# One decoder layer on one core: head squares in four column strips, a priority on the turned keys, and a merge written into the tail of the last scan group

## The chip, the cores and the metric

The kernel runs on one core of a Trainium2 chip. The metric is the device time of one execution in microseconds (us); lower is better.

## The reference

One layer of a hybrid decoder is computed in float32 for a prompt of 512 tokens and for 8 samples of 8 tokens each (576 tokens together), with shared weights:

```python
h = x + 0.5 * swiglu(rmsnorm(x), ffn1)                  # 1024 -> 2816 -> 1024
z, xbc, dt, q, k, v, f, g_ssd, g_att = split(rmsnorm(h) @ w_in)
y_ssd = SSD(z, conv(xbc), dt)                           # 32 heads of 64, 4 groups, state 128
q = rmsnorm(q per head of 64);  k = rmsnorm(k per head of 64)   # 16 query heads, 4 key heads
y_att = attention(q, k_all, v_all, bias from cumsum(log_sigmoid(f)))   # samples: + 2048 cached rows
merged = sigmoid(g_ssd) * (y_ssd @ w_ssd_proj) + sigmoid(g_att) * (y_att @ w_attn_proj)
h = h + merged @ w_out
y = h + 0.5 * swiglu(rmsnorm(h), ffn2)
```

Besides `y`, the keys, values, log forgets and the states of the scan and the convolution are outputs.

## The kernel before

Activations lie turned: 128 features on the partitions, the 576 tokens along the free axis, and eight such tiles make the 1024 features. Each large product is taken in three terms by `mm3` (lines 204 to 210): weights and activations are split in a high part and a remainder of type float32r (`split` and `hilo`; the high part is copied on ScalarE, the remainder subtracted on VectorE, or for some weights on GpSimd), and three matmuls of 128x288 are issued for each 128 rows of the contraction. `acc()` gives such a product a PSUM bank: from two banks called `acc`, and where `wide` is set also from two called `pv`.

A scheduler sets the order on each engine: it simulates the written program and gives each engine one fixed list, in which a block under `soon()` has a higher priority. Within the attention loop the order on TensorE is that of the code (`manual_schedule`). Engines follow their lists strictly; a DMA issue that waits for a buffer holds up what stands behind it on its queue (ScalarE's and GpSimd's DMAs stand in the lists of those engines). Pools hand out tiles by tag; a tile of a tag with `bufs=n` waits until the n-th tile before it is no longer read, and a new pool's tile waits for the tiles whose memory it takes over.

The stages in order of time, with the lines that the change touches:

- FFN 1, until about 470 us.
- Keys, queries and values, 480 to 580 us. Each of ten tiles (2 of keys, 8 of queries; each holds two heads of 64 rows) goes through `squares` (651): ScalarE squares it into `sq`, and two matmuls with a 20-column selector `hE` add the two heads' sums to rows 2j and 2j+1 of `hp_` (512 prompt columns) and `hq_` (64 sample columns). When all ten are in, the 20 rows are turned, their inverse roots are taken on VectorE and turned back into `hr` (20 x 576).
- Heads are scaled by a matmul of `hr` with a selector `sel` that GpSimd copies out of the identity (`heads`, 662): lines 670 and 747 for the keys, 776 for the samples' part of the eight query tiles. These selectors take turns in four buffers.
- Attention, 620 to 900 us. The samples' cached keys `kk` are turned on TensorE (907) and copied to `kT` on ScalarE (908); the scores read them (917). Between these steps `fill()` puts slices of other projections.
- The convolution and four scan groups, 900 to 1390 us. `conv_tile` evicts a projection into `xr` (two buffers) and works on it. Of group g, `group_out` multiplies the scan's output by 512 rows of `w_ssd_proj`: for each of eight tiles j and two halves, twelve matmuls, then VectorE scales the result (`u`, line 1378) and adds it to `accs[j]` (1380).
- The merge, from 1392 us: for each j, two loads (`th` and `mt`, 1403 and 1405), VectorE's `th = (th + 1) * accs[j]` (1406), GpSimd's `th += mt` (1407; VectorE for j = 7), ScalarE's high part `mh` (217), VectorE's remainder `ml` (218). `th` and `mt` come from the pool `mg`, whose memory belongs to the scan's pools before. Then the product with `w_out` (eight tiles, each over all eight `mh` and `ml`) is added to the residual `hts`, which was loaded on ScalarE's queue (1410), and FFN 2 follows, until the end.

Of the kernel before, what the change touches and what calls it, by code (L numbers as in the profile page):

```python
# [48 lines left out]
for _n, _w in (("id", P), ("one", P), ("mT", P), ("smT", NS), ("sgn", 1),  # L49
               ("ev", 1), ("od", 1), ("kb", 4), ("hE", 38), ("scan", NT), ("sm", B * NS), ("rq", 4), ("page", P), ("cm", P)):  # L50
    COFF[_n] = (_o, _w)
    _o += _w
# [3 lines left out]
def constants():  # L56
# [17 lines left out]
    put("kb", ((i[:, None] % 32) // T == np.arange(4)[None]) * 1.0)  # L74
    put("hE", (np.arange(38)[None] == 18 + i[:, None] // 64) * 1.0)
    t = np.arange(NT)
# [17 lines left out]
def build(ctx, tc, A, O):  # L94
# [544 lines left out]
    with pool("att", side="right", reuse_waits="tile") as ap:  # L639
# [9 lines left out]
        nhead = [0]  # L649

        def squares(kf):
# [6 lines left out]
            mm(hp_[:20], lhsT=w, rhs=sq[:, :NP], start=j == 0, stop=j == 9)  # L658
            mm(hq_[:20, :NS], lhsT=w, rhs=sq[:, NP:], start=j == 0, stop=j == 9)

        def heads(j, tag="bias", bufs=4):

            sel = tl(ap, [20, 2, 64], tag=tag, bufs=bufs)
            G.tensor_copy(sel, ident[:20, 2 * j:2 * j + 2].unsqueeze(2).to_broadcast([20, 2, 64]))
            return sel.rearrange("k e m -> k (e m)")
# [56 lines left out]
        vtok = tokens(vf, O["v_p"], O["v_s"], "vt")  # L722
        hr = tl(ap, [20, NT], tag="hr")
        V.tensor_scalar(hr[:, :NP], hp_[:20], 1.0 / 64, EPS, ALU.mult, ALU.add)
        V.tensor_scalar(hr[:, NP:], hq_[:20, :NS], 1.0 / 64, EPS, ALU.mult, ALU.add)

        t = tr()
# [3 lines left out]
        xr_ = tl(ap, [P, 100], tag="pb", bufs=2)  # L731
        V.tensor_copy(xr_, t[:, :100])
        yr = rsqrt(xr_, 100, ap, (("L", 4), ("PT", 2), ("Ls", 7)))
        t = tr()
        for c in range(4):
            nc.tensor.transpose(t[:20, c * P:(c + 1) * P], yr[:, c * 20:(c + 1) * 20], ident)
        V.tensor_copy(hr[:, :NP], t[:20])
        t = tr()
        nc.tensor.transpose(t[:20, :P], yr[:, 80:100], ident)
        V.tensor_copy(hr[:, NP:], t[:20, P - NS:P])  # L740
        khat, khs, sels = kfs, [], []
# [30 lines left out]
        for j in range(8):  # L772
            sel = heads(2 + j)
            if j == 0:
                headnorm(qt[0], sel, 64)
            mm(t[:, j * NS:(j + 1) * NS], lhsT=sel, rhs=hr[:, NP:], start=True, stop=True)
# [10 lines left out]
        newb = tl(ap, [P, B, NS], tag="newb")  # L787
        cn = tl(ap, [P, NS], tag="cn")
        nc.scalar.dma_start(out=cn, in_=ap3(cumD, 32 * NT + NP, [(NT, 16), (0, T), (1, NS)]))
# [92 lines left out]
        class Sample:  # L882
# [17 lines left out]
            def turn_keys(self, jq):  # L900
                kk = self.kk.pop(jq)
                self.kT = []
                for p in range(2):
                    self.kT.append(tl(ap, [P, 512], tag="kT", bufs=2))
                    t = tr()
                    for i in range(4):
                        nc.tensor.transpose(t[:, i * P:(i + 1) * P], kk[:, i, p * P:(p + 1) * P], ident)  # L907
                    act(self.kT[p], t, AF.Copy)

# [187 lines left out]


    xzs = ExitStack()
    xz = xzs.enter_context(pool("xz", side="right", reuse_waits="tile"))  # L1100
# [90 lines left out]

    sa = mixes.enter_context(pool("ssdacc", reuse_waits="tile"))
    with xzs, pool("ssd", side="right", reuse_waits="tile") as wk:
        accs = [tl(sa, [P, NT], tag=f"accs{j}") for j in range(8)]
# [12 lines left out]
        def group_scan(g, bT, cT, xg):  # L1207
# [21 lines left out]
            def halves(half):  # L1229

                for i in range(4):
                    if half == 0:
                        yhl.append((tl(wk, [P, NT], F32R, tag="ygh", bufs=4), tl(wk, [P, NT], F32R, tag="ygl", bufs=4)))
# [130 lines left out]
        def group_out(g, ysq, ys_):  # L1364
# [3 lines left out]
            for j in range(8):  # L1368
                w = cw.get(j)
                for half in range(2):  # L1370
# [5 lines left out]
                    else:  # L1376
                        u = tl(wk, [P, HT], tag="u", bufs=2)
                        V.tensor_tensor(u, a, rg[:, hs(half)], ALU.mult)
                        E = V if g == 3 else G
                        E.tensor_tensor(accs[j][:, hs(half)], accs[j][:, hs(half)], u, ALU.add)  # L1380

        gs = Cols(win, CGS)
        late = iter(range(8))
        for g in range(4):
# [11 lines left out]
    hp2 = ctx.enter_context(pool("h2", side="right", reuse_waits="tile"))  # L1396
    hts = [tl(hp2, [P, NT], tag=f"h{k}") for k in range(8)]
    with mixes:
        with pool("mhl", bufs=8, side="right", reuse_waits="tile") as mp, pool("mg", side="right", reuse_waits="tile") as mg:
            mhl = []  # L1400
            for j in range(8):
                th = tl(mg, [P, NT], tag="th", bufs=3)
                nc.sync.dma_start(out=th, in_=thD[:, 8 + j, :])
                mt = tl(mg, [P, NT], tag="mt", bufs=3)
                nc.scalar.dma_start(out=mt, in_=mattD[:, j, :])
                V.scalar_tensor_tensor(th, th, 1.0, accs[j], ALU.add, ALU.mult)
                (G if j < 7 else V).tensor_tensor(th, th, mt, ALU.add)
                mhl.append(hilo(mp, th, "mh", "ml"))
            for j in range(8):
                nc.scalar.dma_start(out=hts[j], in_=hD[:, j, :])  # L1410
            wide[0] = True
            co = Cols(A["w_out"][0], 0)
            nrm3 = Norm(16, mg)
            for j in range(8):
                w = co.get(j)
                for half in range(2):
                    a = acc()
                    mm3(a, w, mhl, half)
                    hv = hts[j][:, hs(half)]
                    with soon():  # L1420
                        V.scalar_tensor_tensor(hv, a, 0.5, hv, ALU.mult, ALU.add)
                nrm3.add(hts[j])
            nrm3.finish()
            share[0] = 0

# [50 lines left out]
```

## Time and profile before

| | us |
|---|---|
| three runs | 1902.23, 1907.57 (median), 1909.16 |
| profiled execution | 1901.34, of which the span is 1899.5 |
| TensorE busy in the span | 1843.6 (97%) |
| VectorE, ScalarE, GpSimd busy | 1061.9, 745.5, 603.7 |
| mean clock that the throttle granted to TensorE | 0.987 |

PE is TensorE (PEld its weight loads), DVE VectorE, ACT ScalarE, POOL GpSimd, SP the engine that only issues DMAs; a "q" behind a name is an engine's queue. A busy PE is counted by its matmuls' durations, which overlap: neighbours among the 128x288 matmuls start 0.13 us apart and are listed with 0.29 us. "Granted clock" is the share of full speed that TensorE was allowed in a stretch.

### The profile page before, as it was taken

The page shows a single profiled execution, that of the slowest core. Times are in us where ns is not written, and L with a number is a line of the kernel's source. Part 1 is how long each engine was busy: PE and PEld are TensorE (multiplying, and loading weights), DVE is VectorE, ACT ScalarE, POOL GpSimd, SP SyncE. Part 2 cuts the span into 40 slices and gives each one's busy share as a digit, 9 for nine tenths or more (in the row PEclk, how much of TensorE's full clock was granted, in tenths as well). Part 3 has the DMA queues.
Part 4 walks back from the last instruction along what each step waited for, and adds up shares of the span by engine and source line. Part 5 has one row for each costly group of instructions (what it writes and reads, how often), then busy time and mean ns, then how long its engine had stood idle before and what let it go on. Part 6 is the DMA issues. An engine that isn't in the chain of part 4 may idle for free.

```text
span 1899.5 us, 38775 instructions
## 1 busy us (share of the span) xinstructions
PE 1843.6 (97%) x15335; PEld 1738.3 (92%) x15335; DVE 1061.9 (56%) x2308; ACT 745.5 (39%) x1545; POOL 603.7 (32%) x678
## 2 busy tenths in 40 slices
PE   7999999999999999999899999999979999999999
PEld 7999999999899888888898898888979999999998
DVE  5544234443425677776746968787665545445442
ACT  4233223333323555554425645555423333223322
POOL 0432002312312334433224644747434322102210
PEclk9999999999998999999999999999989999999999
DMA  5453443444625678785456445344543444444432
GB/s 153 111 142 123 134 128 118 122 140 140 158 80 147 187 225 244 213 227 155 115 134 190 148 126 144 104 133 123 165 144 109 132 128 139 132 139 123 121 116 69
DMA packets 298235, 269.71 MB, mean 142 GB/s; under 512 B 55068, under 2 KB 262092, under 8 KB 297900
## 3 DMA queue, kind: packets, MB, share of 16 engines
q1 hardware_dynamic: 230864, 186.52, 35.0%
q10 hardware_dynamic: 57828, 46.09, 7.9%
q0 software_dynamic: 9360, 34.61, 5.9%
q8 instruction: 121, 1.98, 0.4%
q14 instruction: 62, 0.51, 0.1%
HBM read 223.71 MB, written 38.73 MB: 138 GB/s over the span
## 4 chain that ended last, share of the span: by engine, by line
PE 85%; DVE 5%; DMA 4%; ACT 3%; issue 1%; POOL 1%; ACTq 1%; SPq 0%; POOLq 0%; DVEq 0%
PE acc L208 17%; PE acc L209 16%; PE acc L210 16%; PE pv L209 7%; PE pv L208 7%; PE pv L210 7%; PE tr L917 2%; PE tr L907 1%; PE mm L844 1%; DMA ab<-cumD 1%; PE pv L875 1%; PE mm L862 1%; PE pv L1299 1%; DVE kf L1140 1%; PE pv L955 1%
## 5 line engine op out<-in xcount | busy, mean ns | idle before, releaser
L173 ACT ACTIVATE whi<-stage 128x512 fp32r<-128x512 f32 (+2 forms) x474 | 294.8, 622 | 739.4 <-PE acc L209 650.5
L208 PE MATMUL acc<-xh,whi 128*128 128x288 f32 x1792 | 544.7, 304 | 9.0 <-ACT tt L1129 3.8
L209 PE MATMUL acc<-xl,whi 128*128 128x288 f32 x1792 | 535.8, 299 | 0.0
L210 PE MATMUL acc<-xh,wlo 128*128 128x288 f32 x1792 | 535.0, 299 | 0.0
L174 DVE TENSOR_TENSOR wlo<-stage,whi 128x512 fp32r<-128x512 f32 (+1 forms) x373 | 261.1, 700 | 263.3 <-ACT whi L173 249.4
L208 PEld LDWEIGHTS acc<-xh,whi 128*128 128x128 f32 x1792 | 341.1, 190 | 15.4 <-ACT tt L1129 6.7
L209 PEld LDWEIGHTS acc<-xl,whi 128*128 128x128 f32 x1792 | 341.3, 190 | 1.9 <-issue 1.4
L210 PEld LDWEIGHTS acc<-xh,wlo 128*128 128x128 f32 x1792 | 340.7, 190 | 1.8 <-issue 1.2
L174 POOL TENSOR_TENSOR wlo<-stage,whi 128x512 fp32r<-128x512 f32 (+1 forms) x101 | 138.2, 1368 | 315.8 <-ACT whi L173 300.4
L341 POOL TENSOR_TENSOR u<-u,s 128x288 f32<-128x288 f32 x88 | 81.3, 924 | 425.6 <-DVE u L340 379.9
L208 PE MATMUL pv<-xh,whi 128*128 128x288 f32 (+1 forms) x720 | 214.1, 298 | 1.0 <-ACT xh L220 0.9
L209 PE MATMUL pv<-xl,whi 128*128 128x288 f32 (+1 forms) x720 | 212.9, 296 | 0.0
L210 PE MATMUL pv<-xh,wlo 128*128 128x288 f32 (+1 forms) x720 | 212.4, 295 | 0.0
L208 PEld LDWEIGHTS pv<-xh,whi 128*128 128x128 f32 (+1 forms) x720 | 135.1, 188 | 1.7 <-ACT xh L220 1.1
L209 PEld LDWEIGHTS pv<-xl,whi 128*128 128x128 f32 (+1 forms) x720 | 135.1, 188 | 1.2
L210 PEld LDWEIGHTS pv<-xh,wlo 128*128 128x128 f32 (+1 forms) x720 | 135.0, 188 | 0.2
L208 PE MATMUL pv<-hh,whi 128*128 128x288 f32 x352 | 105.7, 300 | 0.0
L343 POOL TENSOR_TENSOR hl<-u,hh 128x288 fp32r<-128x288 f32 x88 | 79.1, 901 | 80.7 <-ACT hh L342 80.7
L208 PE MATMUL acc<-hh,whi 128*128 128x288 f32 x352 | 104.1, 296 | 0.0
L209 PE MATMUL pv<-hl,whi 128*128 128x288 f32 x352 | 104.0, 296 | 0.0
L210 PE MATMUL acc<-hh,wlo 128*128 128x288 f32 x352 | 104.0, 296 | 0.0
L209 PE MATMUL acc<-hl,whi 128*128 128x288 f32 x352 | 104.0, 295 | 0.0
(346 smaller groups left out, 3622.5 us busy)
## 6 DMA issues: line engine op xcount, KB each, us to landing
stage<-in_w_in_dram SPq DMA_DIRECT2D x52, 512.0 KB
stage<-in_ffn_w_up_dram SPq DMA_DIRECT2D x44, 512.0 KB
stage<-in_ffn_w_gate_dram SPq DMA_DIRECT2D x43, 512.0 KB
stage<-in_ffn_w_down_dram SPq DMA_DIRECT2D x40, 512.0 KB
h<-in_state_ssm_dram SPq DMA_DIRECT2D x64, 256.0 KB
hTD<-hT ACTq DMA_DIRECT2D x32, 256.0 KB
pb<-pastD SPq DMA_DIRECT2D x32, 256.0 KB
ab<-cumD SPq DMA_DIRECT2D x32, 256.0 KB
```

The lines of the kernel that those rows point to most:

```text
L173: act(hi, view, AF.Copy)
L174: e.tensor_tensor(lo, view, hi.bitcast(F32), ALU.subtract)
L208: mm(out, lhsT=hi, rhs=a, start=first and i == 0, stop=False)
L209: mm(out, lhsT=hi, rhs=b, start=False, stop=False)
L210: mm(out, lhsT=lo, rhs=a, start=False, stop=last and i == n - 1)
L341: G.tensor_tensor(u, u, sil[half], ALU.mult)
L343: G.tensor_tensor(hl[:, hs(half)], u, hh[:, hs(half)].bitcast(F32), ALU.subtract)
L844: mm(s[:, :n], lhsT=q, rhs=ks[2 * self.p + e][:, :n], start=hl == 0, stop=hl == 1)
L862: nc.tensor.transpose(t[:, j * P:(j + 1) * P], lt[:, j * P:(j + 1) * P], ident)
L875: mm(self.ob[o:o + 32, i * P:(i + 1) * P], lhsT=vtok[j][:, v0:v0 + 32], rhs=self.pts[e][:, j * P:(j + 1) * P], start=j == 0, stop=j == i)
L907: nc.tensor.transpose(t[:, i * P:(i + 1) * P], kk[:, i, p * P:(p + 1) * P], ident)
L917: mm(s[kv * 32:(kv + 1) * 32, :], lhsT=self.q(kv), rhs=self.kT[kv // 2], start=True, stop=True)
```

## The change

It has five parts.

1. `squares` writes the squares of a tile to tiles of their own (`sqp` for the prompt, `sqs` for the samples), and does the matmuls only after every fourth tile and after the tenth: tile j goes to the column strip j % 4 (32 columns of the array, 32 rows of the bank), so three batches with 4, 4 and 2 strips replace ten pairs of matmuls on the same 20 columns. The sums lie in rows 32c + 2m; all 128 rows are turned, and six rows of each strip are kept, so `hr` has 24 rows.
2. The selectors of the eight query tiles are copied at once into `sel8`.
3. The copy of the turned keys to `kT` stands under `soon()`.
4. `xr` has three buffers.
5. The merge's loads take their tiles from the pool of the convolution (tags `bT`, `cT`, `xr`), which now stays open; two of them are written ahead of the last `group_out`. The residual is loaded on GpSimd's queue into new tiles of the tags `accs`. All loads of `th` and `mt` are on ScalarE's queue. The scheduler may place merge and last projection among each other.

```diff
         def squares(kf):
             j = nhead[0]
             nhead[0] += 1
-            sq = tl(tp, [P, NT], tag="sq", bufs=1)
-            act(sq, kf, AF.Square)
-            w = C("hE")[:, 18 - 2 * j:38 - 2 * j]
-            mm(hp_[:20], lhsT=w, rhs=sq[:, :NP], start=j == 0, stop=j == 9)
-            mm(hq_[:20, :NS], lhsT=w, rhs=sq[:, NP:], start=j == 0, stop=j == 9)
+            sqp.append(tl(ap, [P, NP], tag="Ls", bufs=7))
+            act(sqp[j], kf[:, :NP], AF.Square)
+            act(sqs[:, j, :], kf[:, NP:], AF.Square)
+            if j % 4 < 3 and j < 9:
+                return
+            for out, sq in ((hp_, lambda i: sqp[i]), (hq_[:, :NS], lambda i: sqs[:, i, :])):
+                for i in range(j // 4 * 4, j + 1):
+                    c, m = i % 4, i // 4
+                    mm(out[c * 32:(c + 1) * 32], lhsT=C("hE")[:, 18 - 2 * m:50 - 2 * m], rhs=sq(i), start=m == 0, stop=i > 5)
...
         for c in range(5):
             o0 = c * P if c < 4 else NT - P
-            nc.tensor.transpose(t[:, c * 20:(c + 1) * 20], hr[:, o0:o0 + P], ident[:20, :20])
+            nc.tensor.transpose(t[:, c * P:(c + 1) * P] if c < 4 else t2[:, :P], hs_[:, o0:o0 + P], ident)
...
+        sel8 = tl(ap, [24, 8, 2, 64], tag="vv", bufs=3)
+        for j, n in ((2, 2), (4, 4), (8, 2)):
+            o = row_of(j)
+            G.tensor_copy(sel8[:, j - 2:j - 2 + n], ident[:24, o:o + 6 * n].rearrange("k (q r) -> k q r", r=6)[:, :, :2]
+                          .unsqueeze(3).to_broadcast([24, n, 2, 64]))
...
-            sel = heads(2 + j)
+            sel = sel8[:, j].rearrange("k e m -> k (e m)")
...
-                    act(self.kT[p], t, AF.Copy)
+                    with soon():
+                        act(self.kT[p], t, AF.Copy)
...
-        xr = tl(xz, XR, tag="xr", bufs=2)
+        xr = tl(xz, XR, tag="xr", bufs=3)
...
+        def merge_load(j):
+            th = tl(xz, [P, NT], tag="cT" if j % 2 else "bT", bufs=2)
+            nc.scalar.dma_start(out=th, in_=thD[:, 8 + j, :])
+            mt = tl(xz, XR, tag="xr", bufs=3)[:, :NT]
+            nc.scalar.dma_start(out=mt, in_=mattD[:, j, :])
+            return th, mt
...
-            group_out(g, *gated)
...
+            if g < 3:
+                group_out(g, *gated)
+    merging = [merge_load(j) for j in range(2)]
+    group_out(3, *gated)
...
+    with mixes, xzs, pool("mhl", bufs=8, side="right", reuse_waits="tile") as mp:
+        mhl, hts = [], []
+        for j in range(8):
+            if j > 1:
+                merging.append(merge_load(j))
+            th, mt = merging[j]
+            V.scalar_tensor_tensor(th, th, 1.0, accs[j], ALU.add, ALU.mult)
+            (G if j < 7 else V).tensor_tensor(th, th, mt, ALU.add)
+            mhl.append(hilo(mp, th, "mh", "ml"))
+            hts.append(tl(sa, [P, NT], tag=f"accs{j}"))
+            nc.gpsimd.dma_start(out=hts[j], in_=hD[:, j, :])
```

Lines behind the first edit move: 670 is 680 in the changed kernel, 747 is 764, 776 is 793, 1378 and 1380 are 1397 and 1399, 1406 is 1432, 1407 is 1433; the selector matmuls of `squares` are line 666.

**The squares on TensorE.** In the changed program the first batch stands in the middle of a projection (`acc<-xh` and `acc<-xl` are its matmuls, `Ls` and `kk` hold the squares). Before, a tile's pair:

```order
L210 MATMUL acc_5638<-xh_4986,wlo_5605 128x288
L208 MATMUL acc_5638<-xh_5086,whi_5608 128x288
L658 MATMUL pv_5532<-sq_5599,cst_75 20x512
L659 MATMUL mm_5533<-sq_5599,cst_75 20x64
L209 MATMUL acc_5638<-xl_5087,whi_5608 128x288
```

Now, the first three strips of the first batch:

```order
L210 MATMUL acc_5858<-xh_4792,wlo_5824 128x288
L666 MATMUL pv_5532<-Ls_5600,cst_75 32x512
L666 MATMUL mm_5533<-kk_5534,cst_75 32x64
L208 MATMUL acc_5858<-xh_4892,whi_5823 128x288
L666 MATMUL pv_5532<-Ls_5664,cst_75 32x512
L209 MATMUL acc_5858<-xl_4893,whi_5823 128x288
L666 MATMUL mm_5533<-kk_5534,cst_75 32x64
L210 MATMUL acc_5858<-xh_4892,wlo_5824 128x288
L208 MATMUL acc_5858<-xh_4986,whi_5823 128x288
L209 MATMUL acc_5858<-xl_4987,whi_5823 128x288
L666 MATMUL pv_5532<-Ls_5738,cst_75 32x512
L666 MATMUL mm_5533<-kk_5534,cst_75 32x64
```

There are still 20 matmuls of these shapes. No two 512-column strips stand next to each other, here or in the other two batches; they stand in twelve places where there were ten.

**The heads' scaling on TensorE.** Before, behind the keys' four matmuls and two for the queries the rest come one by one:

```order
L747 MATMUL mm_6429<-hr_6384,bias_6419 128x64
L747 MATMUL mm_6429<-hr_6384,bias_6424 128x64
L776 MATMUL mm_6460<-hr_6384,bias_6461 128x64
L776 MATMUL mm_6460<-hr_6384,bias_6467 128x64
L210 MATMUL acc_6707<-xh_4792,wlo_6624 128x288
L208 MATMUL acc_6707<-xh_4892,whi_6623 128x288
```

Now all eight follow each other, and the first query tile's prompt part stands behind them:

```order
L680 MATMUL tr_6444<-hr_6423,bias_6442 128x512
L764 MATMUL mm_6447<-hr_6423,bias_6437 128x64
L764 MATMUL mm_6447<-hr_6423,bias_6442 128x64
L793 MATMUL mm_6478<-hr_6423,vv_6433 128x64 x8
L680 MATMUL tr_6479<-hr_6423,vv_6433 128x512
L209 MATMUL acc_6709<-xl_4893,whi_6625 128x288
```

Behind this row stand 41 matmuls of the projection, one transposition, and 120 more.

**The merge on VectorE.** Before, its first rows stand behind the last of the projection's sums:

```order
L1380 TENSOR_TENSOR accs_2343_12683<-accs_2343_12683,u_17747 128x288
L1406 SCALAR_TENSOR_TENSOR th_17769<-th_17769,accs_2336_12676 128x576
L1406 SCALAR_TENSOR_TENSOR th_17779<-th_17779,accs_2337_12677 128x576
L218 TENSOR_TENSOR ml_17776<-th_17769,mh_17775 128x576
L1406 SCALAR_TENSOR_TENSOR th_17789<-th_17789,accs_2338_12678 128x576
```

Now they stand among them, from the first tile on:

```order
L1399 TENSOR_TENSOR accs_2332_12681<-accs_2332_12681,u_17503 128x288
L174 TENSOR_TENSOR wlo_17619<-stage_17616,whi_17618 128x512
L1432 SCALAR_TENSOR_TENSOR bT_17436<-bT_17436,accs_2332_12681 128x576
L1397 TENSOR_TENSOR u_17523<-acc_17510,ssq_16668 128x288
L1399 TENSOR_TENSOR accs_2333_12682<-accs_2333_12682,u_17523 128x288
L1397 TENSOR_TENSOR u_17539<-acc_17526,ssq_16668 128x288
L1399 TENSOR_TENSOR accs_2333_12682<-accs_2333_12682,u_17539 128x288
L1432 SCALAR_TENSOR_TENSOR cT_17440<-cT_17440,accs_2333_12682 128x576
L1397 TENSOR_TENSOR u_17561<-acc_17548,ssq_16668 128x288
L218 TENSOR_TENSOR ml_17770<-bT_17436,mh_17769 128x576
```

On TensorE the last projection's 192 matmuls are followed, and from the sixth tile on mixed, with matmuls of `w_out`; 264 rows of the two stand ahead of the first that reads the eighth `mh`. In the list of ScalarE the copies to `kT` keep their places within the attention loop. In the list of GpSimd the loads of the residual stand behind each tile's addition.

More of the change, by code (lines that the diff above doesn't have):

```diff
@@ L49 @@
 for _n, _w in (("id", P), ("one", P), ("mT", P), ("smT", NS), ("sgn", 1),
-               ("ev", 1), ("od", 1), ("kb", 4), ("hE", 38), ("scan", NT), ("sm", B * NS), ("rq", 4), ("page", P), ("cm", P)):
+               ("ev", 1), ("od", 1), ("kb", 4), ("hE", 50), ("scan", NT), ("sm", B * NS), ("rq", 4), ("page", P), ("cm", P)):
     COFF[_n] = (_o, _w)
@@ L649, in build @@
         nhead = [0]
+        sqs = tl(ap, [P, 10, NS], tag="kk", bufs=3)
+        sqp = []
         def squares(kf):
@@ L787, in build @@
         newb = tl(ap, [P, B, NS], tag="newb")
-        cn = tl(ap, [P, NS], tag="cn")
+        cn = tl(ap, [P, NS], tag="Ln", bufs=2)
         nc.scalar.dma_start(out=cn, in_=ap3(cumD, 32 * NT + NP, [(NT, 16), (0, T), (1, NS)]))
@@ L1096, in build @@
                 G.tensor_copy(yt[p * 4 + g][:, NP:], ys[:, p, g, :])
+    sa = ctx.enter_context(pool("sums", side="right", reuse_waits="tile"))
     xzs = ExitStack()
@@ L1189, in build @@
                 nc.scalar.dma_start(out=mattD[:, j, :], in_=mt)
-    sa = mixes.enter_context(pool("ssdacc", reuse_waits="tile"))
-    with xzs, pool("ssd", side="right", reuse_waits="tile") as wk:
+    wo = xzs.enter_context(pool("outs", side="right", reuse_waits="tile"))
+    with pool("ssd", side="right", reuse_waits="tile") as wk:
         accs = [tl(sa, [P, NT], tag=f"accs{j}") for j in range(8)]
@@ L1376, in group_out @@
                     else:
-                        u = tl(wk, [P, HT], tag="u", bufs=2)
+                        u = tl(wo, [P, HT], tag="u", bufs=2)
                         V.tensor_tensor(u, a, rg[:, hs(half)], ALU.mult)
@@ L1392, in build @@
                 gate_tile(gs, j, 8 + j)
-            group_out(g, *gated)
[L1396 to L1424, printed above, removed]
@@ new lines, in build @@
+            if g < 3:
[13 more added lines that the diff above has]
+            nc.gpsimd.dma_start(out=hts[j], in_=hD[:, j, :])
+        wide[0] = True
+        co = Cols(A["w_out"][0], 0)
+        nrm3 = Norm(16, mp)
+        for j in range(8):
+            w = co.get(j)
+            for half in range(2):
+                a = acc()
+                mm3(a, w, mhl, half)
+                hv = hts[j][:, hs(half)]
+                with soon():
+                    V.scalar_tensor_tensor(hv, a, 0.5, hv, ALU.mult, ALU.add)
+            nrm3.add(hts[j])
+        nrm3.finish()
+        share[0] = 0
```

34 lines of the change are left out of this document (19 added, 15 removed).

## The prediction, before the changed kernel was run

> **What bounds the kernel now.** The page's first part says which engine to follow.
>
> ```profile
> span 1899.5 us, 38775 instructions
> PE 1843.6 (97%) x15335; PEld 1738.3 (92%) x15335; DVE 1061.9 (56%) x2308; ACT 745.5 (39%) x1545; POOL 603.7 (32%) x678
> ```
>
> TensorE fills the span, so an edit pays only where it takes matmul time away, closes an idle stretch, or gives clock back. I then read TensorE's waits (us in total, times, longest):
>
> ```profile
> PE pv L208 <- ACT mh L217: 9.8, 4, 8.1
> PE tr L917 <- ACT kT L908: 5.8, 7, 1.1
> PE acc L208 <- DVE xr L1114: 3.0, 2, 1.8
> ```
>
> Those are the merge, the turned keys and the convolution's eviction, each touched by the change. Last I read stretches: length, PE busy (matmuls), in the first fence the other engines too, then the granted clock, DMA share and GB/s. The first fence is the last `group_out`, the merge, and the rest of `w_out`.
>
> ```profile
> 1367.20:1392.60 25.40, 25.40 (x194) 25.40 (x192) 16.59 (x35) 5.68 (x9) 5.67 (x4) 1.00 0.28 89
> 1392.60:1423.00 30.40, 19.10 (x95) 16.54 (x95) 20.15 (x21) 7.29 (x12) 14.75 (x9) 0.78 0.62 190
> 1423.00:1461.60 38.60, 38.60 (x293) 38.60 (x292) 21.14 (x30) 17.31 (x27) 16.86 (x11) 1.00 0.28 84
> ```
>
> In the third row a matmul costs 38.60 / 293 = 0.132 us. The second row's 95 are worth 12.5 us and took 30.4: the merge loses 17.9 us, partly idle, partly at half clock. The first row loses nothing.
>
> The second fence is the heads' scaling, in steps of 3.41 us.
>
> ```profile
> 584.48:587.89 3.41, 3.41 (x22) 1.00 0.11 40
> 587.89:591.31 3.42, 3.42 (x17) 1.00 0.72 153
> 591.31:594.72 3.41, 3.41 (x14) 0.52 0.13 47
> 594.72:598.13 3.41, 3.41 (x13) 0.50 0.89 227
> 598.13:601.55 3.42, 3.42 (x13) 0.50 0.88 191
> 601.55:604.96 3.41, 3.41 (x16) 0.50 0.25 90
> 604.96:608.37 3.41, 3.41 (x26) 0.98 0.51 139
> ```
>
> TensorE is never idle here, and yet four steps run at half clock: 13.65 us, of which half, 6.8 us, is lost. The fall follows a step full of matmuls with only 20 rows; the rise follows the one step that holds none.
>
> **Part 1, the squares.** Start, duration, engine and line; then the samples' scores, four 32-column strips side by side.
>
> ```profile
> 486.32 0.29 PE L208 MATMUL acc<-xh,whi 128*128 128x288 f32 x1
> 486.54 1.03 PE L658 MATMUL pv<-sq,cst 128*20 128x512 f32 x2
> 487.41 0.28 PE L659 MATMUL mm<-sq,cst 128*20 128x64 f32 x2
> 487.61 0.40 PE L209 MATMUL acc<-xl,whi 128*128 128x288 f32 x1
> ...
> 625.02 0.99 PE tr L917 x8
> ```
>
> A pair occupies 486.45 to 487.61, 1.16 us, ten pairs 11.6 us. Four strips in a row cost 0.99 us, as much as one pair's prompt half. Three such batches would cost some 3 x (0.99 + 0.2 for 64 columns + 0.2 at the borders) = 4.2 us and save 7.4. But in the built order no two 512-column strips are neighbours: a pair on the same strip, or a full-width matmul that needs every column, stands between. So I take no gain. Two more breaks of 0.2 us and five transpositions that now stream 128 columns instead of 20 cost about 1 us. Bounds: +7.4 if the strips overlap nonetheless, -2. Twice as many ScalarE squares hide under its 39% share; without that cover ten times 0.2 us would come on top.
>
> **Part 2, the selectors.** The eight 64-column matmuls move into one burst.
>
> ```profile
> 583.62 1.98 PE L670 MATMUL tr<-hr,bias 20*128 20x512 f32 x4
> 585.44 0.55 PE L747 MATMUL mm<-hr,bias 20*128 20x64 f32 x4
> 585.83 0.60 PE L776 MATMUL mm<-hr,bias 20*128 20x64 f32 x4
> ...
> 589.83 0.29 PE L208 MATMUL acc<-xh,whi 128*128 128x288 f32 x1
> 590.05 0.43 PE L776 MATMUL mm<-hr,bias 20*128 20x64 f32 x2
> 590.41 0.40 PE L209 MATMUL acc<-xl,whi 128*128 128x288 f32 x1
> ```
>
> A lone one costs 590.41 - 589.83 - 0.13 = 0.45 us, in a group 0.25 to 0.3. Six lone ones grouped save about 1 us at full clock. The clock matters more. The burst lasts some 1.8 + 0.5 + 8 x 0.27 + 0.9 = 5.4 us, longer than one step, so I expect the fall; but 41 full matmuls follow, 9.8 us at half clock, and within them lies one whole dense step after which the clock rises. That makes two or three slow steps for four: 1.7 to 3.4 us back. I take 2.5 + 1 = 3.5 us; bounds -1 (a fifth slow step) and 6.8 + 1 = 7.8 (no fall). GpSimd's copies need no data and are early.
>
> [...]
>
> **Part 3, turned keys.** The 5.8 us would be the gain, but the copies keep their places in ScalarE's list, so nothing moves: 0, with 5.8 and -1 as ends.
>
> **Part 4, third `xr` buffer.** The evictions now stand ahead of the previous tile's arithmetic in VectorE's list, so the 3.0 us of waits on `xr` can go. Behind the longer wait the clock falls:
>
> ```profile
> 1153.40 0.40 PE L208 MATMUL acc<-xh,whi 128*128 128x288 f32 x1 [1.84 <-DVE xr L1114]
> ```
>
> What is late next is the tile's own arithmetic. I take half, 1.5 us, between 0 and 3.0 + 1.7 (half of one step).
>
> **Part 5, the merge.** Before, the loads are issued only when the projection has freed the memory (SP and ScalarE queues):
>
> ```profile
> 1391.75 1.41 SPq L1403 DMA_DIRECT2D th<-thD  x3
> 1392.85 1.30 ACTq L1405 DMA_DIRECT2D mt<-mattD  x3
> ```
>
> Now seven of the sixteen stand ahead of the projection, and tile j can be merged once its sum is done. The 17.9 us are the most that this can return. What may replace the load wait is the two engines that share the work:
>
> ```profile
> 1369.51 0.46 DVE L1380 TENSOR_TENSOR accs<-accs,u 128x288 f32<-128x288 f32 x1
> 1371.46 0.68 DVE L174 TENSOR_TENSOR wlo<-stage,whi 128x512 fp32r<-128x512 f32 x1
> 1395.54 0.76 DVE L1406 SCALAR_TENSOR_TENSOR th<-th,accs 128x576 f32<-128x576 f32 x1 [1.70 <-DMA th<-thD]
> 1398.83 2.75 POOL L1407 TENSOR_TENSOR th<-th,mt 128x576 f32<-128x576 f32 x2 [3.86 <-DMA mt<-mattD]
> 1407.11 1.43 POOL L1407 TENSOR_TENSOR th<-th,mt 128x576 f32<-128x576 f32 x1 [2.31 <-DVE th L1406]
> 1407.32 1.83 DVE L1406 SCALAR_TENSOR_TENSOR th<-th,accs 128x576 f32<-128x576 f32 x1 [0.34 <-DMA th<-thD]
> 1409.29 0.76 DVE L218 TENSOR_TENSOR ml<-th,mh 128x576 fp32r<-128x576 f32 x1
> 1361.64 1.29 POOL L174 TENSOR_TENSOR wlo<-stage,whi 128x512 fp32r<-128x512 f32 x1 [5.29 <-ACT whi L173]
> 1408.57 0.68 ACT L217 ACTIVATE mh<-th 128x576 fp32r<-128x576 f32 x1 [3.05 <-POOL th L1407]
> ```
>
> The same `th` operation takes 0.76 us alone and 1.83 beside a GpSimd addition: it ends 0.6 us after the addition does. So I count the two engines' two-input work as one queue. For one tile: two sums 0.92, `th` 0.76, `ml` 0.76, addition 2.75 / 2 = 1.37, and every other tile a split on each engine, 0.34 and 0.65: 4.8 us. TensorE needs 24 x 0.132 = 3.2 us for a tile. Eight tiles are 38.4 us; the first sum starts 2.3 us behind the first matmul (1369.51 against 1367.2), tile 7 adds on VectorE (0.6 less), and its `ml` follows its `mh`: the last `mh` is ready at 2.3 + 38.4 - 0.6 - 0.76 + 0.68 = 40.0 us. The 264 matmuls ahead of its first reader take 34.8. TensorE thus loses 5.2 us, in waits of about 1 us for a bank or an `ml`, too short for the clock, and some 0.3 for the last `ml`. I take 5.5: the gain is 17.9 - 5.5 = 12.4 us. ScalarE's loads for tiles 4 to 7 wait for a remainder two tiles back and are read ten or more us later. The eight residual loads are prepared on GpSimd, where no plain load was seen; nearest is a gather:
>
> ```profile
> 695.02 0.98 POOL L801 DMA_INDIRECT kk<-in_cache_k_dram,pidx  x1 [1.81 <-PE tr L907]
> ```
>
> At 1 us each they fit: GpSimd has 4.8 - 1.37 - 0.65 = 2.8 us free per tile. If they too belong to the queue, 8 us go. So the term lies between 4.4 and 17.9. SP loses its `th` issues; the sample states' loads move ahead of the last two stages of `w_out` there, needed over 20 us later.
>
> [...]
>
> **Sum.** -1 + 3.5 + 0 + 1.5 + 12.4 = 16.4 us off the profiled execution (1901.3: 1899.5 of span and 1.8 around it), 1884.9. The median of the runs, 1907.6, stands 6.2 above that execution; on it the forecast is 1891.2 us.
>
> **Rivals.** A, the forecast: 1891, own range 1886 to 1897, chance 0.45.
>
> B, more comes back: no fall of the clock at the heads (4.3 more), or no queue between the two engines (5.5 more): 1887 or 1886, both 1881. For it: TensorE is busy throughout the burst, and operations reading PSUM (0.46 us for `u`) were not lengthened. Against: 1.83 us, and four slow steps. Chance 0.2; the clock alone has half of that.
>
> C, the merge only moves the stall into the projection. `u` frees a bank and now queues behind `th`; with two banks a delay over 1.6 us stops TensorE. If the residual loads join the queue and the waits cluster until the clock falls, part 5 gives 0 to 5 us, all together 1 to 9: 1899 to 1906. For it: 1.8 idle us in a 3.4 us step sufficed at 1153. Against: GpSimd's slack. Chance 0.27.
>
> D, slower: a residual load holds GpSimd longer than its 2.8 us of slack. The gain of 16.4 is gone at 2.8 + 16.4 / 8 = 4.9 us each, and from 6.1 us the kernel is over 0.5% slower, near 1918 at 6.2. Against: the gather's 0.98 us. Chance 0.08.
>
> E, the change does not do what it says: that is in the forecast for the strips and the keys. If it holds for the merge too, C's time results.
>
> **How the numbers follow.** 0.5%, 9.5 us, is about what a measurement of this kernel tells from no change (its three runs span 6.9 us). Faster by more (under 1898.0): nearly all of A, B, and a little of C, 0.69. Same: most of C and edges of A, 0.22. Slower: D and a rest of C, 0.09. The range reaches from B's 1881 to most of C, 1904; about 2 in 10 are outside.
>
> **What would show it.** Right: TensorE's wait for `mh` of 8.1 us gone, half clock near 1400 gone, waits of about 1 us between the matmuls of the last projection; some 11 to 12 us still spent on the squares; two or three slow steps at the heads; `kT` waits unchanged near 5.8 us. Wrong: `th` at 0.76 us throughout (B), half clock within the projection (C), or GpSimd's loads over 3 us (D).

## The result, and the profile after

The changed kernel runs in 1891.21 us (median of 7 runs, 1889.14 to 1893.85) against 1907.57 us (7 runs, 1898.08 to 1909.96). The ratio is 0.9924, with a 95% interval of 0.9906 to 0.9942: 14.5 us less, give or take 3.4. The forecast was 1891.2 us. Whether it was right in more than the number has to be read term by term: the two profiled executions differ by only 11.1 us of span.

First, the span and the engines in the page of the changed kernel:

```profile
span 1888.4 us, 38769 instructions
PE 1834.7 (97%) x15335; PEld 1729.5 (92%) x15335; DVE 1062.6 (56%) x2309; ACT 746.2 (40%) x1555; POOL 606.5 (32%) x681
```

The bound is the same, and so is the number of matmuls. Then TensorE's waits in the changed kernel (us in total, times, longest):

```profile
PE tr L935 <- ACT kT L926: 5.2, 6, 1.1
PE acc L208 <- DVE u L1397: 3.8, 4, 1.2
...
PE acc L208 <- DVE xr L1133: 2.9, 2, 1.8
...
PE pv L209 <- DVE ml L218: 0.6, 1, 0.6
```

The wait for `mh` (8.1 us at its longest) is gone. In its place stand four waits for `u`, of 0.6 to 1.2 us, inside the last projection. The waits for `kT` and `xr` are nearly what they were (5.8 and 3.0 us before).

Both programs issue the same 15335 matmuls, so the k-th of the one can be set against the k-th of the other. These are the 400 matmuls around the merge (from the 11500th to the 11900th), before, with the columns of the prediction's first stretches (length; busy time of PE, PEld, DVE, ACT and POOL; granted clock; DMA share; GB/s):

```profile
1365.22:1436.30 71.08, 59.78 (x403) 57.22 (x401) 47.11 (x69) 20.53 (x33) 26.34 (x17) 0.90 0.44 139
```

and after:

```profile
1365.90:1424.91 59.01, 54.56 (x402) 53.27 (x401) 49.90 (x69) 20.85 (x33) 30.65 (x27) 1.00 0.63 191
```

The merge gives back 71.08 - 59.01 = 12.1 us. A dense 400 would take 400 x 0.132 = 52.8 us, so 6.2 us are still lost, 4.4 of them in the waits for `u` and `ml` above. The same count from the 3440th to the 4500th matmul covers squares, heads and the first page of keys. Before:

```profile
476.77:633.96 157.19, 157.16 (x1063) 140.44 (x1065) 67.25 (x154) 52.13 (x92) 42.14 (x51) 0.96 0.49 133
```

and after, with the steps around the burst of selectors below it:

```profile
477.49:632.38 154.89, 153.06 (x1062) 136.62 (x1064) 66.29 (x155) 52.57 (x102) 41.74 (x46) 0.99 0.50 135
...
588.21:591.63 3.42, 3.42 (x25) 2.66 (x25) 3.33 (x7) 2.22 (x4) 0.88 (x2) 1.00 0.53 119
591.63:595.04 3.41, 3.41 (x17) 3.41 (x16) 3.25 (x12) 0.63 (x1) 1.83 (x3) 0.50 0.67 190
595.04:598.45 3.41, 3.26 (x25) 3.00 (x24) 3.31 (x9) 0.97 (x2) 0.06 (x1) 1.00 0.48 154
```

One step at half clock is left of four, and the stretch is 2.3 us shorter. The rest of the span adds up to little: +0.7 us ahead of the 3440th matmul, +2.3 in the attention loop (273.9 to 276.2), 0.0 from there to the 11500th, +0.3 behind the merge. All together -11.1.

### The profile page after: what moved, and what is told of

It is laid out like the page before. It is cut to its first block, busy times and chain, and to the rows that moved or that the text cites. A ratio compares the mean times of both kernels' runs of the same rounds, so it can differ in the third digit from the quotient of the medians.

```text
span 1888.4 us, 38769 instructions
## 1 busy us (share of the span) xinstructions
PE 1834.7 (97%) x15335; PEld 1729.5 (92%) x15335; DVE 1062.6 (56%) x2309; ACT 746.2 (40%) x1555; POOL 606.5 (32%) x681
## 4 chain that ended last, share of the span: by engine, by line
PE 83%; DVE 7%; DMA 3%; ACT 3%; issue 2%; POOL 1%; ACTq 1%; SPq 0%; DVEq 0%; POOLq 0%
PE acc L208 16%; PE acc L209 16%; PE acc L210 15%; PE pv L209 8%; PE pv L208 8%; PE pv L210 7%; PE tr L935 2%; PE tr L924 1%; PE mm L861 1%; DMA ab<-cumD 1%; PE pv L892 1%; DVE kf L1159 1%; PE mm L879 1%; PE pv L973 1%; PE tr L376 1%
```

## The experiments

Each run is compared with runs of the kernel before on the same chip. Where a stretch is named, it is the one of the same matmuls as above.

**The merge part alone, on the kernel before.** The edit is the part of the change's diff from the pools `sums` and `outs` to the interleaved loop, and the third `xr` buffer; squares, selectors and keys stay.

```diff
-    sa = mixes.enter_context(pool("ssdacc", reuse_waits="tile"))
+    sa = ctx.enter_context(pool("sums", side="right", reuse_waits="tile"))
...
-            group_out(g, *gated)
+            if g < 3:
+                group_out(g, *gated)
+    merging = [merge_load(j) for j in range(2)]
+    group_out(3, *gated)
...
```

> The kernel before with the merge part alone (pools moved, two tiles loaded ahead of group_out(3), merge interleaved, residual loads on GpSimd, and the third xr buffer that its loads use). Theory: the merge's 17.9 us become some 6 us of waits on VectorE (u) within the last projection, nothing else moves: 12 us faster, ratio about 0.9937, waits of xr still 3.0 us, four slow steps at the heads as before. Rival 1: the part pays less without the rest of the change (the last mh late, the clock falls within the projection): under 6 us. Rival 2: the third buffer also takes the xr waits: 14 to 15 us, xr wait near 0.

Measured: 0.9928 (0.9905 to 0.9952). The merge stretch, and the heads' stretch of the same execution:

```profile
1372.85:1431.87 59.02, 54.62 (x402) 53.34 (x401) 49.87 (x69) 20.84 (x33) 30.35 (x27) 1.00 0.64 191
477.66:637.86 160.20, 160.17 (x1063) 142.26 (x1065) 68.04 (x154) 52.18 (x92) 42.69 (x51) 0.94 0.46 131
```

59.02 us, as in the changed kernel to 0.01. The `xr` wait stayed at 3.0 us. So the merge part alone accounts for the measured ratio, and both rivals fall. Which piece of that part carries the gain (the early loads, the place among the projection's sums, the queues) was not tried apart. The heads here show six slow steps where the profile of before shows four, with the same code there: their number differs from one execution to another.

**The selectors alone, on the kernel before.**

```diff
+        sel8 = tl(ap, [20, 8, 2, 64], tag="vv", bufs=3)
+        G.tensor_copy(sel8, ident[:20, 4:20]...to_broadcast([20, 8, 2, 64]))
-            sel = heads(2 + j)
+            sel = sel8[:, j].rearrange("k e m -> k (e m)")
```

> The kernel before with one tile of eight selectors, still 20 rows, and nothing else of the change. Theory: the grouped 64-column matmuls alone end the run of slow steps: one or two at half clock near 591 to 598 where there were four, 3 to 5 us faster (ratio 0.9975 to 0.998). Rival: the slow steps fell away through the squares' new layout (24 rows, other moments in the 3.41 us grid): four slow steps stay, 0 to 1 us.

Measured: 0.9992 (0.9973 to 1.0011), which tells no gain from none. The heads' stretch:

```profile
475.13:629.38 154.25, 152.68 (x1062) 136.75 (x1064) 67.21 (x154) 52.15 (x92) 40.91 (x44) 0.98 0.50 136
```

Two slow steps, 2.9 us less than the four-step execution and 5.9 less than a six-step one. The slow steps went as expected, the time did not: this execution's attention loop took 278.0 us against 273.9. In the six profiled programs whose attention loop is written as before (one with the keys' copies in front) it took 273.7 to 278.0 us, so the changed kernel's 276.2 is within what that loop does without the change. A gain of 3 us at the heads is thus seen in the profile and not in the time. The grouping also brought waits of TensorE for ScalarE that the kernel before does not have there, one of 0.3 us and this one:

```profile
PE tr L909 <- ACT L L682: 1.3, 1, 1.3
```

**The grouped matmuls with 128 rows, on the changed kernel.** The head tile and its selectors get 104 rows of zeros.

```diff
-        hr = tl(ap, [24, NT], tag="hr")
+        hr = tl(ap, [P, NT], tag="hr")
+        G.memset(hr, 0.0)
...
-        sel8 = tl(ap, [24, 8, 2, 64], tag="vv", bufs=3)
+        sel8 = tl(ap, [P, 8, 2, 64], tag="vv", bufs=3)
```

> The changed kernel with the head tile and its selectors widened from 24 to 128 rows, the added rows zero: the same matmuls in the same order. Theory: what the clock follows in a 3.41 us step is the moved columns weighted by the rows in use. The step ahead of the changed kernel's fall at 591 moves some 3200 columns, 1540 when weighted by rows / 128; steps whose weighted sum was 2790 or more did not fall. With 128 rows the step counts 3200: no slow step at the heads, 1.5 to 2 us faster than the changed kernel (1889), half-clock steps in all one fewer. Rival: the clock follows the share of time or the plain number of columns moved: the slow step at 591 stays, 0 us.

Measured: 0.9889 (0.9860 to 0.9919), 1885.24 us. The heads' stretch:

```profile
473.59:624.84 151.25, 149.50 (x1063) 135.17 (x1065) 66.70 (x155) 52.33 (x102) 42.59 (x47) 1.00 0.50 138
```

The slow step is gone, the stretch is 3.6 us shorter, more than the 1.7 us that one slow step costs. The order on TensorE is not quite the same, against what was expected: it differs in 135 places, all in this stretch, and behind the heads the strips of the samples' scores take 1.07 us where they took 1.83. The next run has no such difference. The time against the changed kernel fell by more than the 2 us expected (0.9889 to 0.9924), but the two intervals overlap.

**128 rows alone, on the kernel before**, with the 64-column matmuls left scattered (the same edit, each selector by itself).

```diff
-            sel = tl(ap, [20, 2, 64], tag=tag, bufs=bufs)
-            G.tensor_copy(sel, ident[:20, 2 * j:2 * j + 2]...to_broadcast([20, 2, 64]))
+            sel = tl(ap, [P, 2, 64], tag=tag, bufs=bufs)
+            G.tensor_copy(sel, ident[:, 2 * j:2 * j + 2]...to_broadcast([P, 2, 64]))
...
-        hr = tl(ap, [20, NT], tag="hr")
+        hr = tl(ap, [P, NT], tag="hr")
+        G.memset(hr, 0.0)
```

> The kernel before with the head tile and each selector widened from 20 to 128 rows (the added rows zero) and nothing else: the 64-column matmuls stay scattered. Theory: the clock at the heads follows moved columns weighted by rows. The step ahead of the fall moves 3700 to 3800 columns, 1500 to 2700 when weighted; at 128 rows it counts in full, above the 2500 to 2900 where steps begin to fall, and the steps behind it never start: no slow step at the heads (before: four to six), 7 to 10 us faster than before, ratio 0.995 to 0.9965, more than the grouping alone gave. Rival: the scattered short matmuls themselves lower the clock: four slow steps or more stay, ratio 1.000.

Measured: 0.9956 (0.9939 to 0.9973), as expected. The heads' stretch:

```profile
474.71:623.10 148.39, 148.36 (x1063) 134.53 (x1064) 67.83 (x154) 52.22 (x92) 43.38 (x52) 1.00 0.50 141
```

No slow step, 8.8 us less than 157.19, and the order on TensorE is that of the kernel before in all 15335 places. The scattered order alone thus does not lower the clock. Not all of the 8.8 us is clock: four slow steps are worth 6.8. A lone pair of 64-column matmuls, 0.45 us by the prediction's count, now costs 587.34 - 587.07 - 0.13 = 0.14:

```profile
587.07 0.29 PE L208 MATMUL acc<-xh,whi 128*128 128x288 f32 x1
587.20 0.33 PE L777 MATMUL mm<-hr,bias 128*128 128x64 f32 x2
587.34 0.38 PE L209 MATMUL acc<-xl,whi 128*128 128x288 f32 x1
```

Six such pairs are 1.9 us: the change from 128 rows to 20 and back cost time too.

**The strips as neighbours, on the changed kernel.** The batch is written with the last tile first and kept in that order on TensorE, so that nothing is ready before all four are.

```diff
+            with tc.manual_schedule(engines={mybir.EngineType.PE}):
...
-                for i in range(j // 4 * 4, j + 1):
+                    for i in range(j, j // 4 * 4 - 1, -1):
```

> The changed kernel with the strips of a batch written last tile first and kept in that order on TensorE, so that the four 512-column strips are neighbours in the built order. Theory: scattered strips overlap with nothing; neighbours share TensorE, three batches take some 4 to 5 us instead of 11, and the kernel is 6 to 7 us faster than the changed one (near 1884). Rival 1: strips into one bank do not overlap in this place (another stationary matrix for each, weights of 32 columns): 11 us stay, 0 us. Rival 2: the squares are late when a batch waits for its last one, TensorE idles 1 to 2 us a batch: a gain of 2 us or less.

Measured: 0.9882 (0.9854 to 0.9911), 1882.7 us. Busy time of the squares' matmuls, in the changed kernel:

```profile
L666 PE MATMUL pv<-Ls,cst 128*32 128x512 f32 x20 | 10.5, 604 | 0.0
...
L666 PE MATMUL mm<-kk,cst 128*32 128x64 f32 x20 | 2.8, 221 | 0.0
```

and with neighbours:

```profile
L667 PE MATMUL pv<-Ls,cst 128*32 128x512 f32 x20 | 3.2, 605 | 0.0
L667 PE MATMUL mm<-kk,cst 128*32 128x64 f32 x20 | 0.9, 224 | 0.0
```

Each takes its 0.60 us as before, but four now run at once: 10.5 us of TensorE become 3.2. The heads' stretch falls from 154.89 to 147.33 us although it has two slow steps here, one more than in the changed kernel. With half of each slow step's 3.41 us taken off, an estimate that is called "at full clock" from here on, that is 153.2 to 143.9: 9.3 us that the built order had thrown away. (Before, full matmuls start 0.24 us apart in the slow steps, from 593.11 on, and 0.13 at full clock: a slow step holds 14 of them where a full one holds 26, so the estimate takes off some 0.1 us too much for each step.)

**The squares in pairs again, with merge and selectors** (the kernel before with the two edits above; the keys' copies as there).

> The kernel before with the merge part and the eight grouped selectors (20 rows); the squares stay in pairs, the turned keys' copies as before. Theory: the scattered strips bring nothing (they cost some 1.5 us in the changed kernel), nor do the keys' copies: as fast as the changed kernel or up to 2 us faster, ratio to the kernel before 0.991 to 0.9925. Rival: the strips or the keys' copies carry a part of the gain: 3 us or more slower than the changed kernel, ratio above 0.994.

Measured: 0.9904 (0.9879 to 0.9929), at least as fast as the whole change.

```profile
1361.41:1420.45 59.04, 54.62 (x403) 53.32 (x401) 49.90 (x69) 20.85 (x33) 30.73 (x27) 1.00 0.65 191
477.84:632.06 154.22, 152.56 (x1062) 137.03 (x1064) 66.76 (x154) 52.13 (x92) 41.73 (x44) 0.98 0.50 136
```

At full clock (two slow steps here, one in the changed kernel) the heads' stretch is 154.22 - 3.41 = 150.8 us against 154.89 - 1.71 = 153.2: the scattered strips and their wider transpositions cost 2.4 us.

**The two small edits alone, on the kernel before.**

```diff
-        xr = tl(xz, XR, tag="xr", bufs=2)
+        xr = tl(xz, XR, tag="xr", bufs=3)
...
-                    act(self.kT[p], t, AF.Copy)
+                    with soon():
+                        act(self.kT[p], t, AF.Copy)
```

> The kernel before with the two small edits alone: the third xr buffer and the turned keys' copies in front. Theory: neither does anything. The copies keep their place; the wait on xr's eviction ends late because VectorE works through four ygl operations (3.5 us) ahead of it, not for want of a buffer: xr wait 3.0 us, kT waits 5 to 6 us, ratio 1.000. Rival: the buffer takes the xr wait (0 to 1 us left) and the half-clock step behind it, 3 to 5 us faster; or the keys' copies take some of their 5.8 us.

Measured: 0.9988 (0.9972 to 1.0005), with these waits:

```profile
PE tr L918 <- ACT kT L909: 5.7, 7, 1.1
...
PE acc L208 <- DVE xr L1115: 3.0, 2, 1.8
```

Neither wait moved; in all ten programs with three buffers the two waits for `xr` add up to 2.9 or 3.0 us. Why the buffer does nothing is read from VectorE's list in the changed kernel (start, duration), not tried:

```profile
1151.11 3.52 DVE L1256 SCALAR_TENSOR_TENSOR ygl<-xg,P,ygh 128x288 fp32r<-128x288 f32 x4
1154.56 0.44 DVE L1133 TENSOR_TENSOR xr<-acc,rbc 128x288 f32<-128x288 f32 x1
```

The eviction starts as soon as four splits of the gated output are through. They stand ahead of it on the same engine, and no buffer changes that.

**All additions of the merge on VectorE, on the changed kernel.**

```diff
-            (G if j < 7 else V).tensor_tensor(th, th, mt, ALU.add)
+            V.tensor_tensor(th, th, mt, ALU.add)
```

> The changed kernel with all eight additions of mt in the merge on VectorE instead of seven on GpSimd. Theory: VectorE and GpSimd share one queue for two-input work on memory, so the addition leaves GpSimd (1.4 us) and takes 0.76 us on VectorE, and the sums beside it fall from 0.91 us on the mean to about 0.5: TensorE's waits on u stay within 2 us of the changed kernel's 3.8, the time within 2 us of it. Rival: the engines work side by side and VectorE is simply full: 7 x 0.76 = 5.3 us more work on it, sums still longer than 0.7 us, 4 to 6 us slower than the changed kernel.

Measured: 0.9895 (0.9870 to 0.9920). The merge stretch, and the groups of the sums and the additions in it (busy us, mean ns):

```profile
1362.33:1417.16 54.83, 53.81 (x403) 53.17 (x402) 46.14 (x76) 20.11 (x33) 23.16 (x20) 1.00 0.69 205
...
L1399 DVE TENSOR_TENSOR accs<-accs,u 128x288 f32<-128x288 f32 x16 | 8.7, 554 | 0.1
...
L1433 DVE TENSOR_TENSOR bT<-bT,xr 128x576 f32<-128x576 f32 x4 | 3.0, 748 | 0.0
```

The same groups in the changed kernel:

```profile
L1399 DVE TENSOR_TENSOR accs<-accs,u 128x288 f32<-128x288 f32 x16 | 14.5, 908 | 0.3
...
L1433 POOL TENSOR_TENSOR bT<-bT,xr 128x576 f32<-128x576 f32 x4 | 5.9, 1480 | 11.4 <-DVE bT L1432 6.5 <-issue 5.0
...
L1436 POOL DMA_DIRECT2D accs<-hD x8 | 4.5, 563 | 1.4 <-DVE cT L1432 1.4
```

VectorE took on seven more operations of 0.75 us and its busy time in the stretch fell from 49.90 to 46.14 us: the sums went from 0.91 us each to 0.55. The stretch is 4.2 us shorter, so the rival (an engine simply full) falls. So does the "within 2 us" of the expectation, which was its own theory misread: in one queue an addition costs 1.37 us on GpSimd and 0.76 on VectorE, and 7 x 0.61 = 4.3 us.

**Three tiles merged ahead of the projection.** `(1 + th) * accs + mt` is formed for tiles 0 to 2 before the rowscale, and `u` is multiplied by `(1 + th) * rg`.

```diff
+                    V.scalar_tensor_tensor(accs[j], th, 1.0, accs[j], ALU.add, ALU.mult)
+                    G.tensor_tensor(accs[j], accs[j], mt, ALU.add)
             rg = rowscale(ysq, 1.0 / 512, ysq)
...
+                    V.scalar_tensor_tensor(th, th, 1.0, rg, ALU.add, ALU.mult)
+                    rgs[j] = th
...
-                        V.tensor_tensor(u, a, rg[:, hs(half)], ALU.mult)
+                        V.tensor_tensor(u, a, rgs[j][:, hs(half)], ALU.mult)
```

> The changed kernel with three of the eight tiles merged ahead: before the last projection (1 + th) * accs + mt is formed for tiles 0 to 2, and u is multiplied by (1 + th) * rg there, so that only the sum and its split are left behind the projection. It takes three th operations and three GpSimd additions (some 3 x 2.1 us of the shared two-input time) out of the projection and puts three th-sized operations just ahead of it. Theory: the projection is late by the shared queue, so the 5.9 us that TensorE loses there fall to 1 to 3: 3 to 5 us faster than the changed kernel. Rival 1: the three operations ahead delay the first u: their 2.3 us come back as a wait, 0 to 2 us gained. Rival 2: the loss there comes from the loads (share of the DMA engines 0.58), not from the two engines: unchanged at 6 us.

Measured: 0.9901 (0.9875 to 0.9928).

```profile
1357.93:1412.58 54.65, 53.98 (x402) 53.20 (x401) 44.34 (x66) 20.77 (x33) 26.99 (x24) 1.00 0.70 198
```

4.4 us less than 59.01, in the expected 3 to 5. The share of the DMA engines rose (0.63 to 0.70) while the loss fell, which speaks against the loads as its cause.

**The three edits together** (the diffs of the neighbouring strips, the 128 rows on the changed kernel, and the additions on VectorE), and these with three tiles ahead (additions of the other five on VectorE).

> The changed kernel with neighbouring strips, 128 rows at the heads, and all additions of the merge on VectorE. Theory: the three are independent: 7.5 us at the squares, 2 to 3 at the heads' clock, 4.2 in the merge, 13 to 15 us faster than the changed kernel, near 1876, ratio 0.984 to 0.9855. Rival: the shorter squares only bring the heads up to data that is not there (keys' first page), and half comes back: 7 us, ratio 0.988.

> The same with three tiles merged ahead of the last projection. Theory: the addition on VectorE and the early tiles work on the same 6 us; the former left 2.0 us over the dense 52.8, so at most 2 us more: 1 us faster than the kernel without it, within what is measured. Rival: with both, VectorE is overfull ahead of the projection and the first u waits: 1 to 2 us slower.

Measured: 1867.05 us, 0.9826 (0.9802 to 0.9851), and 1867.08 us, 0.9821 (0.9797 to 0.9845). The first, merge and heads:

```profile
476.32:619.49 143.17, 140.22 (x1063) 132.66 (x1065) 66.65 (x155) 52.42 (x102) 42.40 (x47) 1.00 0.53 146
1350.99:1405.83 54.84, 53.81 (x403) 53.18 (x402) 46.15 (x76) 20.11 (x33) 23.17 (x20) 1.00 0.68 205
```

Against the changed kernel the heads give 11.7 us and the merge 4.2, 15.9 where 13 to 15 were expected, so the rival (half comes back) falls. The ratios say 18.6 us, give or take 6, which agrees. The tiles ahead shorten the merge stretch by another 0.8 us (54.03), which the time does not show. By the medians either version gains more on the changed kernel than the whole change gained on the kernel before.

## Why the prediction was right, and where it was not

**The merge: right, in size and in mechanism.** The term was 12.4 us back out of 17.9, with 5.5 lost to VectorE and GpSimd taking turns. It measured 12.1 back and 6.2 lost, in short waits as forecast, and four other programs repeat the stretch (59.00 to 59.04 us). The sum behind the term holds too. GpSimd's seven additions start 4.74 us apart on the mean, where the prediction had 4.8 us for a tile, and the last `mh` is ready 40.5 us behind the projection's first matmul, where it had 40.0:

```profile
1367.90 0.29 PE L208 MATMUL acc<-ygh,whi 128*128 128x288 f32 x1
...
1407.76 0.69 ACT L217 ACTIVATE mh<-cT 128x576 fp32r<-128x576 f32 x1 [2.17 <-DVE cT L1433]
```

What it had wrong is which operation waits. `th`, 1.83 us beside an addition before, took 0.76 us or less throughout in the changed kernel, which was the sign named for rival B. The queue is there all the same; the sums (0.91 us on the mean, 0.46 before) and the remainders (1.37 and 1.02 us, 0.76 alone) bear it:

```profile
L218 DVE TENSOR_TENSOR ml<-cT,mh 128x576 fp32r<-128x576 f32 x4 | 5.5, 1366 | 0.2 <-ACT mh L217 0.2
...
L218 DVE TENSOR_TENSOR ml<-bT,mh 128x576 fp32r<-128x576 f32 x4 | 4.1, 1021 | 0.0
...
L1432 DVE SCALAR_TENSOR_TENSOR cT<-cT,accs 128x576 f32<-128x576 f32 x4 | 3.0, 754 | 0.1
```

A sign should therefore name the engine's whole queue, not one operation of it. That the turns are the cause, and not the loads or a full VectorE, is shown by the two experiments that took two-input work out of the projection or off GpSimd: each returned over 4 of the 6.2 us. In the run with all additions on VectorE the sums' mean fell from 908 to 554 ns when only GpSimd's additions left.

**The squares: right that the strips do not overlap, cost too small.** Forecast -1 with -2 as the lower end; 2.4 us measured. The neighbours' run has 143.9 us at full clock where pairs have 150.8: 6.9 us were to be had (7.4 was the upper end).

**The selectors: the clock returned more than forecast, the grouping nothing in the end.** Forecast 2.5 us by the clock (two or three slow steps left) and 1 us by grouping. One slow step is left in the changed kernel (5.1 us back) and two with the selectors alone (3.4); in the six programs with the burst of 20 or 24 rows it is one or two. At full clock the stretch did not shrink: 154.25 - 3.41 = 150.8 with the selectors alone, against 157.19 - 6.83 = 150.4 before. TensorE's busy time there did fall by the forecast 1 us (152.68 - 3.41 = 149.3 against 157.16 - 6.83 = 150.3), but the new waits of 1.6 us for ScalarE's `L` took it back; the prediction had no term for what the heads would run into when they come earlier. Squares and selectors together were forecast at 2.5 us and measured 2.3.

**The third `xr` buffer: the step failed.** The prediction took half of 3.0 us because the built order put the evictions ahead of the previous tile's arithmetic. The wait behind which the clock fell was for the four `ygl` operations, which the order still has ahead of the eviction. The wait is 2.9 us, the term 0. The step at 1154 ran at full clock in the changed kernel, but one at 926 ran at half clock; of the 13 profiled programs ten have a slow step near 926 and five one near 1150, so one execution does not show that either came or went by the change.

**The keys: right**, 0 of 5.8 us.

**The sum.** 12.1 + 2.3 + 0 + 0 = 14.4 us, and the measured ratio says 14.5. The forecast said 16.4, too much by the `xr` term, and that it hit the median is luck: the medians of the two sets of runs happen to lie 16.4 apart, the profiled executions 11.1. The 2.3 us at the heads also hang on an execution of the kernel before with four slow steps there; with six they would be some 3 us more. Rival B did not come: the queue is there, and one step still fell. Of C, `u` did queue and stop TensorE, for 3.8 us. But C needed the clock to fall within the projection, and it did not: the stretch has clock 1.00. D needed residual loads of over 4.9 us on GpSimd; they took 0.56.

## What to carry to other kernels

Look at the order that is built, not the one that is written: matmuls on disjoint column strips are worth their overlap only as neighbours (here 3.2 us of TensorE side by side against 10.5 apart), and writing the last-ready one first under a fixed order makes them so. Before giving GpSimd a share of VectorE's two-input work on a critical stretch, count both engines as one queue: here each of the seven additions on GpSimd saved VectorE 0.75 us and held it up by (49.90 - 46.14 + 7 x 0.75) / 7 = 1.3. When an eviction is late, read what stands ahead of it on its engine before adding a buffer.

## What was not expected of the hardware

The clock followed more than TensorE's busy time, and the rows in use are part of it. For each step of 3.41 us, spread the moved columns of each matmul from its start to the next one's, and add them up, each times its rows over 128 (a dense step counts 26 x 288, some 7500). Over the 13 profiles, 66 of the 70 falls to half clock came behind a step with a sum under 2900, and no step at full clock with a sum under 2250 was followed by another (the first 24 us and the end left out); between the two both happen. As a threshold alone plain columns do hardly worse: the best one leaves 16 steps on the wrong side, the best for the weighted sum 15. What speaks for the rows are the padded runs. The changed kernel fell to half clock behind a step at 588 of some 3200 columns, busy throughout, of which the weighting leaves 1540. With 128 rows it has a step of some 3040 columns, TensorE idle for 1.55 us of it, and the next step kept full clock:

```profile
591.14:594.55 3.41, 1.86 (x15) 1.62 (x15) 3.27 (x9) 2.33 (x6) 1.30 (x1) 1.00 0.56 154
```

The falls at the heads went in all four programs with the padding (clock 1.00 in the heads' stretch of each). Zero rows thus count as rows. The kernel before is a closer case: it fell behind a step of some 3790 columns, 2710 when weighted, so the step was only in part of 20-row matmuls and not full of them, as the prediction read it. The padding also packs more columns into a step (cheaper pairs, above), so rows were not varied with all else equal. The four exceptions (sums of some 3280 to 3650) all stand at the convolution's eviction near 1140, with 1.8 us idle and narrow strips in the rest of the step; what is counted there stays open.

The granted clock changes in steps of 3.41 us (at the heads the slow stretch of before is 13.65 us long, four steps, that of the changed kernel 3.41), and with the same code at the heads there are four slow ones in one program and six in two others; that this hangs on where the steps begin was not tried. Idle time of TensorE ahead of a fall, 1.84 us at 1153 before, does not cover the heads. Here are the step ahead of the fall and the six slow steps of the run with the two small edits:

```profile
582.95:586.36 3.41, 3.41 (x18) 2.29 (x17) 2.06 (x5) 1.34 (x3) 0.97 (x4) 1.00 0.37 119
586.36:606.85 20.49, 20.49 (x69) 16.34 (x68) 11.47 (x26) 5.07 (x10) 4.73 (x9) 0.50 0.43 118
```

TensorE is busy throughout both, in the second at clock 0.50, where the same matmuls in the same order with 128 rows kept 1.00.
